# A two-layer DiT trunk on one core: attention by pairs of key tiles, modulation by quads

## The chip, the cores and the metric

The kernel runs on one core of a Trainium2 chip. A core has five engines with queues of their own, each of which works its instructions off in order: TensorE (PE in the profile, with the loads of its stationary operand as PEld), VectorE (DVE), ScalarE (ACT), GpSimd (POOL) and SyncE (SP, which here only issues transfers). The metric is the device time of one execution in microseconds (us); less is better.

## What is computed

The reference is a trunk of two layers over 1024 latent and 256 context tokens of width 1024. In each layer the input is normalised and modulated, projected, and sent through four mixers of 256 columns each (mLSTM, attention with low-rank keys and values, a state-space mixer, an S5 scan); their outputs are concatenated, projected and added, and a convolutional FFN follows. Two parts matter here, cut to their lines:

```python
ml = jnp.split(s_lat @ w_mod[l] + b_mod[l], 6, axis=-1)   # modulation, latent
mc = jnp.split(s_ctx @ w_mod[l] + b_mod[l], 6, axis=-1)   # modulation, context
...
def attend(q, k, v):                                       # 4 heads, q and k of 96, v of 64
    s = jnp.einsum('bqhd,bkhd->bhqk', q, k).astype(jnp.float32) * scale
    p = jax.nn.softmax(s, axis=-1).astype(v.dtype)
    return jnp.einsum('bhqk,bkhd->bqhd', p, v)

yc = attend(qc, kc, vc)            # context queries over 256 context keys
yl = attend(ql, k_all, v_all)      # latent queries over all 1280 keys
```

Layer 1 needs no context output, so its attention has latent queries only.

## The kernel before

Activations lie with features on partitions and tokens along the free axis. All is kept in float32; most products are made of three fp32r matmuls on split operands (a high part and a low part, lines 288 to 290), which pass the array once, while a plain float32 product passes it twice.

**Attention.** `attend` (from line 957) goes over two pairs of heads, the two heads `ho` of a pair, and groups of queries `(t0, w)`: in layer 0 256 context queries, then 512 and 512 latent ones; in layer 1 the latter two. A context group meets two tiles of 128 keys, a latent group ten. Ahead of the groups of head h stands `scores(h + 1)`: the key projection of the next head (`a_pkn`, lines 288 to 290) and the maxima of its scores (`a_pm` on PE, line 949, then a reduction on DVE, `a_mx`, line 950); the negated maximum becomes row 96 of the query operand, so that the exponential needs no further subtraction. For each key tile three matmuls (lines 980 to 982) put the scores of 128 keys and w queries into one PSUM bank `a_pst`, ACT takes the exponential into `a_E` (line 984), and one float32 product (line 985) accumulates `a_po`. Its stationary operand is 128 columns of `a_vt`: 64 of values and 64 of ones, so that one half of the rows of `a_po` is the weighted sum and the other the sum of the weights. At the end of a group ACT copies the two halves out (lines 987 and 988); after the second head of a pair DVE takes the reciprocal (line 990), POOL multiplies (line 991), and the result goes to DRAM.

PSUM's eight banks are three pools: `pd` with two banks (`acc`: projections, maxima), `pa` with three (`a_po` and the scores, which so have two banks in turn) and `pb` with three (mLSTM and modulation).

**Modulation.** `mod` (line 140) takes four tiles of 128 output features. The stationary operand is the 32-column `sc`; four of them stand side by side on the array's columns, and a tile of weights `wm` (512 KB, loaded at line 137) is the moving operand: eight matmuls of 128 columns (line 154) for each tile. ACT copies the four column groups out (line 157, `wms`), and a small product with `msel` adds them up (line 159). Layer 0 makes its first 16 tiles ahead of everything; 48 tiles are made within layer 0's attention and 32 within layer 1's. At each group's start and end `extra()` takes the next word of a list PLAN, whose letters stand for one chunk of mLSTM or four tiles of modulation.

**What sets the order.** The kernel is written for a framework that plans the order of each engine's queue at build time: an instruction that is ready by the planner's costs goes first by its place in the program, or by a priority that the code raises. So mLSTM (`m_...`), modulation and the next head's maxima fall between the score and value matmuls on PE. Both layers have a stretch of some 20 us at the end of attention where nothing of these is left.

## Time and profile before

| | us |
|---|---|
| median of 3 runs | 3469.59 (3468.87 to 3469.73) |
| the profiled execution | 3470.5 |
| its span on the core | 3468.7 |
| PE busy in the span | 3246.6 (94%) |
| DVE, ACT, POOL busy | 2047.4, 1244.0, 1081.7 |
| attention of layer 0, by its place in the span | 541 to 870 |
| attention of layer 1 | 2365 to 2650 |

The profile is of one execution. Its rows give, for groups of instructions, the line of the kernel, the engine, the output and inputs by their names in the program, shapes, busy time and mean time; in the timeline each row is a run of like instructions with its start, and records of PE overlap, since matmuls are pipelined: what one costs is read from the starts of its neighbours, not from its own length. A float32 matmul leaves two records, one for each pass. The granted clock (PEclk) is 1.00 at 2.4 GHz.

### The profile page before, as it was taken

How to read it: one execution, taken by the hardware profiler on the slowest of the kernel's cores; microseconds unless marked ns; L12 is line 12 of the kernel's file. 1: busy time of each engine (PE TensorE's matmuls, PEld its weight loads, DVE VectorE, ACT ScalarE, POOL GpSimd, SP SyncE). 2: the span in 40 equal slices, each digit the busy share in tenths (PEclk: the TensorE clock that was granted, in tenths of full speed). 3: DMA queues.
4: the chain of work that ended last, by engine and by line, in shares of the span. 5: the costliest groups of instructions: out<-in, count | busy, mean ns of one | idle time of the engine just before them, and what ended most of it. 6: DMA issues, size and time to landing. Idle time of an engine off the chain costs nothing.

```text
span 3468.7 us, 49086 instructions
## 1 busy us (share of the span) xinstructions
PE 3246.6 (94%) x18567; PEld 2715.2 (78%) x18598; DVE 2047.4 (59%) x3967; ACT 1244.0 (36%) x2149; POOL 1081.7 (31%) x1043
## 2 busy tenths in 40 slices
PE   7899998999989999998999799998999899999996
PEld 6798896666878888886888789996656788887785
DVE  7858647554485333339778583536544855555655
ACT  4223544334344333333111424534334444444211
POOL 1922324011045444442111020223101375554220
PEclk9899999999999999998999899998999999999998
DMA  5566634236412111225332465544153322223421
GB/s 203 159 200 207 178 104 140 91 115 234 156 62 87 66 68 66 73 79 193 112 104 90 128 203 163 154 120 124 60 196 110 106 89 81 84 84 127 147 73 49
DMA packets 287165, 423.63 MB, mean 122 GB/s; under 512 B 91016, under 2 KB 197200, under 8 KB 286928
## 3 DMA queue, kind: packets, MB, share of 16 engines
q1 hardware_dynamic: 176788, 301.29, 28.2%
q10 hardware_dynamic: 110140, 119.20, 10.3%
q8 instruction: 146, 2.39, 0.3%
q14 instruction: 91, 0.75, 0.1%
HBM read 301.48 MB, written 118.91 MB: 121 GB/s over the span
## 4 chain that ended last, share of the span: by engine, by line
PE 39%; DVE 6%; DMA 2%; issue 2%; ACT 1%; SPq 0%; POOL 0%; ACTq 0%; POOLq 0%; DVEq 0%
PE pd L289 4%; PE pd L290 4%; PE pd L288 4%; PE px L288 2%; PE px L290 2%; PE px L289 2%; PE a_po L985 2%; PE ps_in L289 1%; PE ps_in L288 1%; PE ps_in L290 1%; PE pz L288 1%; PE pz L289 1%; PE pz L290 1%; PE ps_out L289 1%; PE ps_out L288 1%
## 5 line engine op out<-in xcount | busy, mean ns | idle before, releaser
L289 PE MATMUL pd<-fl,wh_d 128*128 128x512 f32 (+1 forms) x896 | 333.5, 374 | 15.2 <-DVE fl L206 15.2
L288 PE MATMUL pd<-fh,wh_d 128*128 128x512 f32 (+1 forms) x896 | 326.9, 374 | 20.0 <-ACT fh L205 12.5
L290 PE MATMUL pd<-fh,wl_d 128*128 128x512 f32 (+1 forms) x896 | 328.4, 371 | 0.0
L206 POOL TENSOR_TENSOR wl_d<-wr_d,wh_d 128x1024 fp32r<-128x1024 f32 x44 | 112.3, 2570 | 461.5 <-ACT wh_d L205 366.7
L1647 DVE SCALAR_TENSOR_TENSOR xx<-pd,modv,xx 128x512 f32<-128x512 f32 (+1 forms) x248 | 165.0, 677 | 121.7 <-PE pd L290 121.0
L288 PE MATMUL ps_in<-ha,wh_in 128*128 128x384 f32 (+3 forms) x688 | 217.7, 326 | 17.0 <-ACT st L1473 16.7
L290 PE MATMUL ps_in<-ha,wl_in 128*128 128x384 f32 (+3 forms) x688 | 223.3, 325 | 0.0
L289 PE MATMUL ps_in<-ha,wh_in 128*128 128x384 f32 (+3 forms) x688 | 223.2, 324 | 0.0
L288 PE MATMUL ps_in<-hc,wh_in 128*128 128x256 f32 (+1 forms) x704 | 215.1, 308 | 6.7 <-ACT hc L220 4.5
L289 PE MATMUL ps_in<-hc,wh_in 128*128 128x256 f32 (+1 forms) x704 | 214.7, 305 | 0.7 <-DVE hc L221 0.7
L290 PE MATMUL ps_in<-hc,wl_in 128*128 128x256 f32 (+1 forms) x704 | 214.0, 304 | 0.0
L288 PEld LDWEIGHTS pd<-fh,wh_d 128*128 128x128 f32 x896 | 171.1, 192 | 53.6 <-ACT fh L205 15.2
L289 PEld LDWEIGHTS pd<-fl,wh_d 128*128 128x128 f32 x896 | 172.3, 193 | 47.1 <-DVE fl L206 19.6
L290 PEld LDWEIGHTS pd<-fh,wl_d 128*128 128x128 f32 x896 | 171.8, 192 | 28.1
L950 DVE TENSOR_REDUCE a_mx<-a_pm 128x1 f32<-128x512 f32 (+1 forms) x200 | 114.6, 591 | 116.7 <-PE a_pm L949 115.1
L985 PE MATMUL a_po<-a_E,a_vt 128*128 128x512 f32 (+1 forms) x336 | 171.1, 595 | 2.9 <-ACT a_E L984 2.5
L206 POOL TENSOR_TENSOR wlo_u<-wr_u,whi_u 128x1024 fp32r<-128x1024 f32 x44 | 106.2, 2415 | 216.2 <-ACT whi_u L205 177.0
L984 ACT ACTIVATE a_E<-a_pst 128x512 f32<-128x512 f32 (+1 forms) x168 | 98.3, 587 | 202.7 <-PE a_pst L982 199.7
L205 ACT CAST wh_d<-wr_d 128x1024 fp32r<-128x1024 f32 x44 | 45.2, 1047 | 299.6 <-PE pd L289 193.9
L288 PEld LDWEIGHTS ps_in<-ha,wh_in 128*128 128x128 f32 x688 | 133.0, 194 | 19.7 <-ACT st L1473 17.1
L288 PEld LDWEIGHTS ps_in<-hc,wh_in 128*128 128x128 f32 x704 | 135.7, 194 | 8.8 <-ACT hc L220 5.6
L206 DVE TENSOR_TENSOR wlo_s<-wr_s,whi_s 128x1024 fp32r<-128x1024 f32 x42 | 71.3, 1697 | 118.2 <-ACT whi_s L205 118.2
(637 smaller groups left out, 9425.1 us busy)
## 6 DMA issues: line engine op xcount, KB each, us to landing
...
```

The costliest lines, as they stand in the source:

```text
L205: nc.scalar.copy(hi, src)
L206: (eng or nc.gpsimd).tensor_tensor(lo, src, hi.bitcast(F32), OP.subtract)
L288: mm(ps, whi(k), ahi(k), start=start and i == 0, stop=False)
L289: mm(ps, whi(k), alo(k), start=False, stop=False)
L290: mm(ps, wlo(k), ahi(k), start=False, stop=stop and i == len(ks) - 1)
L950: nc.vector.tensor_reduce(mx[:, c, j:j + 1], ps[:, :kw], mybir.AxisListType.X, OP.max)
L984: nc.scalar.activation(E[:, :w], ps[:, :w], AF.Exp, scale=scale)
L985: nc.tensor.matmul(po[:, :w], vt[:, kt, hp, 64 * ho:64 * ho + P], E[:, :w], start=kt == 0, stop=kt == kts[-1])
L1647: nc.vector.scalar_tensor_tensor(v, ps, K.modv[l][:, 8 * part + m, c:c + 1], v, OP.mult, OP.add)
```

## The change

In attention two key tiles form a pair. Six score matmuls fill a tile of two PSUM banks, one exponential of 128 x 1024 follows, and the value product becomes two float32 matmuls with 64 stationary columns each, tile i of the pair on columns 64 i to 64 i + 63 and so on rows 64 i of `a_po`. The ones in `a_vt` are gone (64 columns for each head, one copy for a chunk of keys where there were two). The sums of the weights are now added up elementwise: POOL adds the first tile of each pair to `S`, DVE the second; after the second head of a pair of heads `finish` adds the two on DVE, two matmuls with 64 columns of ones sum over the partitions (`a_pr`), DVE takes the reciprocal from PSUM, POOL multiplies. The halves of `a_po` are joined by one ACT copy and one DVE addition. PSUM's pool `pa` is closed and opened anew around attention: one bank for `a_po` and one tile of two banks for the scores, so the scores have no second buffer. In `mod_load4` and `mod` four tiles of modulation are loaded into one tile of 2 MB (two of them instead of four of 512 KB) and multiplied by eight matmuls of 512 columns, issued together; the 16 tiles ahead of layer 0 stay as they were. The value products, `a_pr` and these matmuls have a raised priority.

The core of the diff:

```diff
-        self.pd, self.pa, self.pb = (ctx.enter_context(pool_(tc, name=f"p{i}", bufs=b, space=PSUM)) for i, b in (("d", 2), ("a", 3), ("b", 3)))
+        self.pd, self.pb = (ctx.enter_context(pool_(tc, name=f"p{i}", bufs=b, space=PSUM)) for i, b in (("d", 2), ("b", 3)))
+        self.cpa = None
+        ctx.callback(lambda: self.cpa.close())
+        self.open_pa()
...
+        self.cpa = ExitStack()
+        self.pa = self.cpa.enter_context(pool_(self.tc, name=f"p{name}", bufs=3 if name[0] == "a" else 1, space=PSUM))
...
+    def mod_load4(self, l, js, pool, bufs):
+
+        w = pool.tile([P, 4, KT, P], F32, tag="wm", name=f"wm{l}_{js[0]}", bufs=bufs)
+        for i, j in enumerate(js):
+            self.nc.sync.dma_start(w[:, i], self.A["w_mod"][l, j])
+        return w
...
+            if hasattr(ws, "name"):
+                with self.tc.high_priority(TOGETHER):
+                  for r in range(2):
+                    for g in range(4):
+                        nc.tensor.matmul(ps[32 * g:32 * g + 32, :], self.sc[:, 2 * g + r], ws[:, :, 2 * g + r], start=r == 0, stop=r == 1, skip_group_check=True)
+            for i, j in enumerate(() if hasattr(ws, "name") else js):
...
-        vt = self.vt = late.tile([P, NCH, 2, 192], F32, name=n("vt"))
+        vt = self.vt = late.tile([P, NCH, 4, 64], F32, name=n("vt"))
...
-        nc.gpsimd.memset(vt[:, :, :, 64:128], 1.0)
...
-            for o in range(2):
-                nc.scalar.copy(vt[:, c, :, 128 * o:128 * o + 64], psv[:, :, o])
+            nc.scalar.copy(vt[:, c], ps[:, :256].rearrange("p (h e) -> p h e", h=4))
...
-                    po = K.psm.tile([P, 512], F32, tag="m", name=n(f"po{h}{t0}"))
-                    kts = range(2) if t0 < TC else range(NCH)
-                    for kt in kts:
-                        ks = slice(kt * P, kt * P + P)
-                        ps = K.psm.tile([P, 512], F32, tag="m", name=n(f"pst{h}{t0}{kt}"))
-                        nc.tensor.matmul(ps[:, :w], kh[:97, ks], qh[:97, t0:t0 + w], start=True, stop=False)
-                        nc.tensor.matmul(ps[:, :w], kh[:96, ks], ql[:96, t0:t0 + w], start=False, stop=False)
-                        nc.tensor.matmul(ps[:, :w], kl[:96, ks], qh[:96, t0:t0 + w], start=False, stop=True)
-                        E = epool.tile([P, 512], F32, tag="E", name=n(f"E{h}{t0}{kt}"), bufs=3)
-                        nc.scalar.activation(E[:, :w], ps[:, :w], AF.Exp, scale=scale)
-                        nc.tensor.matmul(po[:, :w], vt[:, kt, hp, 64 * ho:64 * ho + P], E[:, :w], start=kt == 0, stop=kt == kts[-1])
-                    me, ot = slice(64 * ho, 64 * ho + 64), slice(64 - 64 * ho, 128 - 64 * ho)
-                    nc.scalar.copy(y[me, :w], po[me, :w])
-                        nc.vector.reciprocal(r[:, :w], r[:, :w])
-                        nc.gpsimd.tensor_tensor(y[:, :w], y[:, :w], r[:, :w], OP.mult)
-                        y_put(2 + hp, 1, y[:, None, :w], t0, w)
...
+                        ys[t0].append(epool.tile([P, 2, 2, w], F32, tag=f"S{t0}", name=n(f"S{hp}{t0}"), bufs=1))
+                    y, r, S = ys[t0]
+                    po = K.pa.tile([P, 512], F32, tag="m", name=n(f"po{h}{t0}"))
+                    nk = 2 if t0 < TC else NCH
+                    old = None
+
+                    def values(k0, E):
+                        with K.tc.high_priority(TOGETHER):
+                          for i in range(2):
+                            nc.tensor.matmul(po[64 * i:64 * i + 64, :w], vt[:, k0 + i, h], E[:, i, :w], start=k0 == 0, stop=k0 + 2 == nk)
+
+                    for k0 in range(0, nk, 2):
+                        ps = K.pa.tile([P, 2, 512], F32, tag="s", name=n(f"pst{h}{t0}{k0}"))
+                        for i in range(2):
+                            ks = slice((k0 + i) * P, (k0 + i) * P + P)
+                            nc.tensor.matmul(ps[:, i, :w], kh[:97, ks], qh[:97, t0:t0 + w], start=True, stop=False)
+                            nc.tensor.matmul(ps[:, i, :w], kh[:96, ks], ql[:96, t0:t0 + w], start=False, stop=False)
+                            nc.tensor.matmul(ps[:, i, :w], kl[:96, ks], qh[:96, t0:t0 + w], start=False, stop=True)
+                        E = epool.tile([P, 2, 512], F32, tag="E", name=n(f"E{h}{t0}{k0}"), bufs=3)
+                        nc.scalar.activation(E[:, :, :w], ps[:, :, :w], AF.Exp, scale=scale)
+                        if old:
+                            values(*old)
+                        if k0 == 2:
+                            settle()
+                        for i in range(2):
+                            if nk == 2:
+                                eng[i].tensor_copy(S[:, i, ho], E[:, i, :w])
+                            elif k0:
+                                eng[i].tensor_tensor(S[:, i, ho], old[1][:, i, :w] if k0 == 2 else S[:, i, ho], E[:, i, :w], OP.add)
+                        old = k0, E
+                    values(*old)
                     nc.scalar.copy(r[me, :w], po[ot, :w])
-                    nc.scalar.copy(y[me, :w], po[me, :w])
+                    nc.vector.tensor_tensor(y[me, :w], po[me, :w], r[me, :w], OP.add)
+
+                    def finish(h=h, t0=t0, w=w, y=y, r=r, S=S, hp=hp):
+                        ps = K.acc(n(f"pr{h}{t0}"))
+                        nc.vector.tensor_tensor(S[:, 0], S[:, 0], S[:, 1], OP.add)
+                        with K.tc.high_priority(TOGETHER):
+                          for i in range(2):
+                            nc.tensor.matmul(ps[64 * i:64 * i + 64, :w], K.ones[:, :64], S[:, 0, i], start=True, stop=True)
+                        nc.vector.reciprocal(r, ps[:, :w])
+                        nc.gpsimd.tensor_tensor(y, y, r, OP.mult)
+                        y_put(2 + hp, 1, y[:, None, :w], t0, w)
+
+                    settle()
                     if ho:
+                        later.append(finish)
                     extra()
+        settle()
...
-                    ready.append((*q, iter(list(K.mod_load(*q, mw, 4)))))
+                    ready.append((*q, K.mod_load4(*q, mw, 2)))
...
+            K.open_pa(f"t{l}")
             at.attend(ap, ep, y_put, extra)
+            K.open_pa(f"a{l}")
```

**PE, end of layer 0's attention.** No filler is left here; `a_pst` are scores, `a_po` value products. Before:

```order
L985 MATMUL a_po_9221<-a_E_9268,a_vt 128x512
L980 MATMUL a_pst_9278<-a_qh_6611,a_kh_6517 128x512
L981 MATMUL a_pst_9278<-a_ql_6615,a_kh_6517 128x512
L982 MATMUL a_pst_9278<-a_qh_6611,a_kl_6519 128x512
L985 MATMUL a_po_9221<-a_E_9275,a_vt 128x512
L980 MATMUL a_pst_9285<-a_qh_6611,a_kh_6517 128x512
L981 MATMUL a_pst_9285<-a_ql_6615,a_kh_6517 128x512
L982 MATMUL a_pst_9285<-a_qh_6611,a_kl_6519 128x512
L985 MATMUL a_po_9221<-a_E_9282,a_vt 128x512
```

Now (lines 1020 to 1022 are the scores, 1014 the values):

```order
L1014 MATMUL a_po_8783<-a_E_8791,a_vt 64x512 x2
L1020 MATMUL a_pst_8793<-a_qh_6600,a_kh_6517 128x512
L1021 MATMUL a_pst_8793<-a_ql_6604,a_kh_6517 128x512
L1022 MATMUL a_pst_8793<-a_qh_6600,a_kl_6519 128x512
L1020 MATMUL a_pst_8793<-a_qh_6600,a_kh_6517 128x512
L1021 MATMUL a_pst_8793<-a_ql_6604,a_kh_6517 128x512
L1022 MATMUL a_pst_8793<-a_qh_6600,a_kl_6519 128x512
L1014 MATMUL a_po_8783<-a_E_8800,a_vt 64x512 x2
L1020 MATMUL a_pst_8813<-a_qh_6600,a_kh_6517 128x512
```

What one key tile did, six scores and a pair of half-width products do; the values of a pair come right ahead of the next pair's scores.

**PE, modulation in layer 1.** `pm` on line 154 is modulation; the names `wm_34` to `wm_36` are its tiles. Before:

```order
L982 MATMUL a_pst_24943<-a_qh_23134,a_kl_23042 128x512
L154 MATMUL pm_32_24959<-wm_34_24880,sc 32x128 x6
L154 MATMUL pm_32_24959<-wm_35_24882,sc 32x128 x2
L949 MATMUL a_pm_24645<-a_kh_23041,a_qh_23135 128x512
L154 MATMUL pm_32_24959<-wm_35_24882,sc 32x128 x2
L954 MATMUL a_pmr_24639<-cst,a_mx_24598 1x128
L985 MATMUL a_po_24886<-a_E_24940,a_vt 128x512
L980 MATMUL a_pst_24950<-a_qh_23134,a_kh_23040 128x512
L981 MATMUL a_pst_24950<-a_ql_23138,a_kh_23040 128x512
L982 MATMUL a_pst_24950<-a_qh_23134,a_kl_23042 128x512
L154 MATMUL pm_32_24959<-wm_35_24882,sc 32x128 x4
L154 MATMUL pm_36_25008<-wm_36_25000,sc 32x128 x4
```

Now, the same tiles (line 172 is modulation, 183 the product with `msel`, 975 the maxima's transposition, 312 to 314 the key projection):

```order
L172 MATMUL pm_32_24454<-wm_32_24380,sc 32x512 x8
L975 MATMUL a_pmr_23828<-cst,a_mx_23741 1x128
L312 MATMUL a_pkn_24134<-a_kvh,a_wkh 64x432
L313 MATMUL a_pkn_24134<-a_kvl,a_wkh 64x432
L314 MATMUL a_pkn_24134<-a_kvh,a_wkl 64x432
L183 MATMUL pm_32_24454<-msel,wms_32_24463 128x2 x4
L172 MATMUL pm_36_24476<-wm_36_24471,sc 32x512 x8
```

Before, each tile's matmuls stand apart between scores and values; now four tiles go as one block, and several such blocks stand close together.

**PE, the last maxima of layer 0** (line 949 before, 970 now). Before:

```order
L949 MATMUL a_pm_8684<-a_kh_6517,a_qh_6611 128x512
L980 MATMUL a_pst_9174<-a_qh_6611,a_kh_6517 128x512
L981 MATMUL a_pst_9174<-a_ql_6615,a_kh_6517 128x512
L982 MATMUL a_pst_9174<-a_qh_6611,a_kl_6519 128x512
L949 MATMUL a_pm_8687<-a_kh_6517,a_qh_6611 128x512
L159 MATMUL pm_4_8912<-msel,wms_4_8945 128x2 x4
L985 MATMUL a_po_9145<-a_E_9171,a_vt 128x512
L980 MATMUL a_pst_9181<-a_qh_6611,a_kh_6517 128x512
L981 MATMUL a_pst_9181<-a_ql_6615,a_kh_6517 128x512
L982 MATMUL a_pst_9181<-a_qh_6611,a_kl_6519 128x512
L949 MATMUL a_pm_8690<-a_kh_6517,a_qh_6611 128x256
L985 MATMUL a_po_9145<-a_E_9178,a_vt 128x512
```

Now:

```order
L970 MATMUL a_pm_8443<-a_kh_6517,a_qh_6600 128x512
L970 MATMUL a_pm_8446<-a_kh_6517,a_qh_6600 128x512
L970 MATMUL a_pm_8449<-a_kh_6517,a_qh_6600 128x256
L970 MATMUL a_pm_8453<-a_kh_6517,a_qh_6600 128x512
L970 MATMUL a_pm_8456<-a_kh_6517,a_qh_6600 128x512
L970 MATMUL a_pm_8459<-a_kh_6517,a_qh_6600 128x256
L970 MATMUL a_pm_8463<-a_kh_6517,a_qh_6600 128x512
L970 MATMUL a_pm_8466<-a_kh_6517,a_qh_6600 128x512
L970 MATMUL a_pm_8469<-a_kh_6517,a_qh_6600 128x256
L975 MATMUL a_pmr_8473<-cst,a_mx_8374 1x128 x3
L1044 MATMUL a_pr_8498<-a_S_7638,ones 64x512 x2
L975 MATMUL a_pmr_8473<-cst,a_mx_8374 1x128
```

The maxima stood one by one between scores and values, and now stand in one run that ends with the sums `a_pr` (line 1044) and a block of modulation.

## Rows read from the trace of the kernel before

**Rows 1.** windows: start:end, length, busy us (instructions) by engine, granted clock, DMA share, rate.

```profile
541.00:870.00 329.00, 313.23 (x2076) 212.80 (x2084) 189.68 (x405) 133.21 (x272) 57.82 (x62) 0.96 0.43 139
2365.00:2650.00 285.00, 271.36 (x1552) 175.00 (x1561) 155.62 (x326) 113.00 (x214) 43.15 (x44) 0.96 0.37 120
```

**Rows 2.** page, section 5: group | busy us, mean ns | idle before, releaser.

```profile
L950 DVE TENSOR_REDUCE a_mx<-a_pm 128x1 f32<-128x512 f32 (+1 forms) x200 | 114.6, 591 | 116.7 <-PE a_pm L949 115.1
L985 PE MATMUL a_po<-a_E,a_vt 128*128 128x512 f32 (+1 forms) x336 | 171.1, 595 | 2.9 <-ACT a_E L984 2.5
...
L984 ACT ACTIVATE a_E<-a_pst 128x512 f32<-128x512 f32 (+1 forms) x168 | 98.3, 587 | 202.7 <-PE a_pst L982 199.7
```

**Rows 3.** the waits in layer 0: us in total, times, longest.

```profile
PEld a_po L985 <- ACT a_E L984: 3.1, 3, 1.4
```

**Rows 4.** timeline in the end of layer 1: start, length, engine, line, operation.

```profile
2631.74 0.40 PE L982 MATMUL a_pst<-a_qh,a_kl 96*128 96x512 f32 x1
...
2631.97 1.02 PE L985 MATMUL a_po<-a_E,a_vt 128*128 128x512 f32 x2
2632.17 0.60 ACT L984 ACTIVATE a_E<-a_pst 128x512 f32<-128x512 f32 x1 [1.21 <-PE a_pst L982]
...
2632.43 0.80 PE L980 MATMUL a_pst<-a_qh,a_kh 97*128 97x512 f32 x1
...
2633.07 0.39 PE L981 MATMUL a_pst<-a_ql,a_kh 96*128 96x512 f32 x1
```

**Rows 5.** timeline of PE in layer 1, modulation between maxima.

```profile
2532.72 0.43 PE L154 MATMUL pm<-wm,sc 128*32 128x128 f32 x8
2533.07 0.50 PE L949 MATMUL a_pm<-a_kh,a_qh 96*128 96x512 f32 x1
2533.50 0.85 PE L154 MATMUL pm<-wm,sc 128*32 128x128 f32 x20
...
2534.60 0.63 PE L154 MATMUL pm<-wm,sc 128*32 128x128 f32 x12
2535.16 0.33 PE L824 MATMUL m_pf<-cst,m_h 128*128 128x128 f32 x1
2535.41 0.64 PE L154 MATMUL pm<-wm,sc 128*32 128x128 f32 x14
```

**Rows 6.** windows, modulation alone (operands named wm): PE busy (matmul records).

```profile
541.00:870.00 329.00, 34.28 (x768) 22.97 (x768) 0.96 0.43 139
2365.00:2650.00 285.00, 25.71 (x512) 15.09 (x512) 0.96 0.37 120
```

**Rows 7.** timeline of PE, mLSTM products of 64 stationary columns, then the next product.

```profile
526.29 0.66 PE L748 MATMUL m_pu<-m_vw,m_kt 128*64 128x130 f32 x8
526.89 0.44 PE L737 MATMUL m_pt<-cst,m_lk 128*128 128x128 f32 x2
```

**Rows 8.** lines by form: count, ns least/median/most, first and last start.

```profile
L205 ACT CAST wh_d<-wr_d x44: 1031/1047/1056, 1530.2 to 3411.1; 128x1024 fp32r<-128x1024 f32 x44
...
L1760 DVE TENSOR_TENSOR xx<-xx,xr x40: 409/685/2875, 1588.0 to 3233.2; 128x512 f32<-128x512 f32 x32, 128x256 f32<-128x256 f32 x8
...
L1830 POOL TENSOR_TENSOR wr_s<-wr_s,wr_u x42: 1287/2156/2551, 1033.3 to 3135.3; 128x512 f32<-128x512 f32 x42
```

**Rows 9.** timeline, layer 0: last exponential, load for its product, next stage.

```profile
861.50 0.60 ACT L984 ACTIVATE a_E<-a_pst 128x512 f32<-128x512 f32 x1 [0.97 <-PE a_pst L982]
...
862.15 0.30 PEld L985 LDWEIGHTS a_po<-a_E,a_vt 128*128 128x128 f32 x2 [0.72 <-ACT a_E L984]
...
864.98 1.75 PE L288 MATMUL ps_out<-hb,wh_out 128*128 128x256 f32 x4 [1.70 <-ACT hb L205]
```

**Rows 10.** windows after layer 0, and within layer 1; columns as in rows 1.

```profile
865.00:870.00 5.00, 4.98 (x20) 4.19 (x20) 5.00 (x3) 3.90 (x6) 4.64 (x4) 0.66 0.85 304
875.00:880.00 5.00, 2.77 (x13) 1.97 (x14) 2.63 (x2) 3.75 (x6) 3.31 (x3) 1.00 1.04 397
...
2563.00:2573.00 10.00, 9.96 (x49) 6.07 (x48) 5.23 (x12) 4.52 (x7) 0.00 (x0) 1.00 0.90 346
```

14 lines of the change are left out of this document (11 added, 3 removed).

## The prediction

> **What bounds the kernel now.** I read the windows of the two attention stages first: PE is busy 313.2 of 329 us in layer 0 and 271.4 of 285 in layer 1, the next engine, DVE, 189.7 and 155.6 [rows 1]. Then the page's groups and the waits, which say from which side an operation is late: the exponential idles 199.7 us for the scores on PE, the value product idles 2.9 us in all, 3.1 us of waits in layer 0 [rows 2, 3]. So PE sets the time of both stages, ACT is ahead of it, and the change is worth what it takes off PE less the waits it puts there. Outside the stages the instructions are the same. The sum is made against the profiled 3470.5 us; the median lies 0.9 lower.
>
> **Prices on PE.** They are read from starts [rows 4]: the last score matmul and the first value pass are 0.23 apart; from the value product's start to the start of the next second score matmul it is 1.10, so the product's two passes cost 1.10 - 0.23 = 0.87. A key tile costs 3 x 0.23 + 0.87 = 1.56, a pair 3.12. From the last score matmul's start the exponential begins after 0.43 [rows 4], and the load for its product 0.05 after the exponential's end [rows 9]. An exponential of 512 columns takes 0.60 [rows 4]; one of 1024 is not in the trace. It lies between ACT's 1024-column cast, 1.05 [rows 8], and two exponentials, 1.20; I take 1.05, as it is one instruction over the same length.
>
> **Value products.** Do two products on halves of the columns run side by side? Eight passes of mLSTM products with 64 columns and 130 moving elements are followed by the next product after 0.60 us [rows 7]. One pass of 130 costs 0.87 / 1024 x 130 = 0.11, so eight in turn need 0.88 and two abreast 0.44; they run abreast, and about 0.16 is an overhead. What entering and leaving such a block costs shows better in modulation [rows 5]: 2532.72 to 2533.50 is 0.78; two rounds of four (8 records) take 2 x 0.109 and the maximum between 0.235, so 0.33 is left. 2534.60 to 2535.41 leaves 0.81 - 0.33 - 0.11 = 0.37. I take 0.33 (0.16 to 0.37).
>
> The trace shows a loss of about a third of a us for each block that splits the columns [rows 5]. The Trainium skill (TensorEngine Tiling (Array Packing), Key Properties) says that changing the tiling mode drains TensorE, which speaks against many small blocks. By its two-times speedup alone (Theoretical Speedup) a pair would save 0.87 and not 0.54, an estimate from that page that would put the kernel some 28 us lower. The trace agrees with the drain, and the sum does without that page.
>
> A pair then costs 0.87 + 0.33 for its values where two products took 1.74: 0.54 saved, **if other work covers the exponential**. Scores have one buffer, and the values stand right ahead of the next scores, so between the last score and the values PE needs filler of 0.43 + 1.05 + 0.05 - 0.23 = 1.30 us. I counted the filler of each pair in the new PE order at the trace's prices. Of 80 pairs of 512 queries, 56 have it, 7 have part (short by 0.35 on average), and 17 have none: the ends of both stages (8 and 9 pairs), as in the first order fence. Covered: 56 x 0.54 = -30.2. Part: 7 x (0.54 - 0.35) = -1.3. Without cover a pair is 5 x 0.23 + 0.43 + 1.05 + 0.05 + 0.87 + 0.33 = 3.88 against 3.12, so 17 x 0.76 = +12.9. The four context pairs: +0.5.
>
> **Sums of the weights.** `finish` adds ten blocks, eight of 0.87 + 0.33 and two of half the length: +11.1.
>
> **Modulation.** The stages hold 768 and 512 records [rows 6]; at four abreast that is 1280 / 4 x 0.109 = 34.9 us of streaming, and the new matmuls of 512 columns stream the same. What goes are blocks: I count some 43 and 45 runs in the timeline (from 647.3 and 2493.2 on), and 12 and 8 in the new order. 68 x 0.33 = -22.4 (with 0.16 to 0.37: -11 to -25).
>
> The parts on PE come to -29.4.
>
> **What comes back.**
> - The end of layer 0. Before, 33 matmuls of the next stage lie in the last value products, and even so PE waits 1.70 us for ACT's `hb` afterwards [rows 9]. In the new order all of them follow the last values. They are some 6 us at 0.12 to 0.23 each, part of which fills waits for transfers there: +4 (0 to 8). The same in layer 1 stood behind before, too.
> - The runs of maxima (third fence). DVE takes 0.59 for a maximum [rows 2], PE 0.12 to 0.23, and two banks are between them; a run of 14 holds PE some 14 x (0.59 - 0.19) = 5.6 us, less the other work in it. Transfers: in layer 1 the last four quads of modulation are 8.4 MB close together (second fence); the best rate in that stage is 346 GB/s [rows 10], so 24 us against some 22 of PE work between them. Both together +8 (2 to 14): these are the only rows that touch it, so the middle.
> - The additions to `S`: 64 on DVE at 0.69 and 64 on POOL at 1.29 at the least [rows 8], stand in DVE's queue ahead of maxima. 64 x 0.69 = 44 us fit into DVE's 269 idle us of the two stages [rows 1], as do the 8 additions of 1024 columns. POOL is idle most of the time. The exponentials lose their double buffer on PSUM, so an ACT instruction ahead of them now costs PE where it cost nothing. +3 for both (0 to 14; the upper end is the second rival).
> - At no cost: the copies of `a_vt` (ten ACT instructions fewer), the addition of the halves on DVE (some 20 of 0.6), three buffers for `a_E` of twice the size. DVE's idle covers these; if it were the bound they would cost some 10 us.
>
> -29.4 + 15 = -14.4: 3456.1 in a profile, 3455.2 in the median.
>
> **Rivals.**
> - *All covered.* The returns do not arise, since runs of maxima and exponentials' waits hide each other: -29 to -25, so 3440 to 3445. For it: PE waited only 3 us for exponentials though ACT was not idle [rows 3]. Against it: that was with two score buffers.
> - *DVE and POOL block each other.* POOL's addition of 128 x 512 with two SBUF inputs takes 1.29 at its best and 2.16 in the median, DVE's 0.69 in the median and 2.88 at the worst [rows 8], so each has a partner that stretches it. In the change both start right after the same exponential. If DVE's waits for POOL's, 64 x 1.29 = 83 us come on DVE: its share in the stages rises from 56% to (345 + 44 + 83 + 10) / 600 = 80%, and maxima behind an addition are late by up to 2 us. With 40 pairs that have maxima as filler and a quarter of that reaching PE, 40 x 0.5 = 20, of which 3 is in the sum: 3472, no change. The Trainium skill (SBUF — State Buffer, Who interferes with whom) states that a DVE instruction with two SBUF inputs and a GpSimd instruction that reads SBUF hold a shared port pair in turn, each for its whole length; the rows' stretched times agree, and no row shows it for these operations.
> - *PE's clock falls in the ends.* PE then waits about 1.5 us in each of 17 to 24 pairs that are not covered. After 2.5 us of idleness at the end of layer 0 the granted clock was 0.66 over 865 to 870, a mix of 1.2 and 2.4 GHz [rows 10]. At the lower level a pair's 1.15 + 1.20 us of PE work double: +2.35, and 17 to 24 pairs give +40 to +56 us: **slower**, 3495 to 3511, from the point at which more than six of them run so. Against it: over 875 to 880, with PE busy 2.77 of 5 us, the clock stayed 1.00 [rows 10], and in the ends it would be busy about 2.4 of 3.9.
> - *The halves do not run abreast* for 512 moving elements: 84 x 0.87 + 10 x 0.87, +80, 3535. The rows of 130 elements speak against it [rows 7].
>
> **How the numbers follow.** My forecast, 3446 to 3462, has 0.42; all covered (3425 to 3446) 0.17; DVE and POOL (3462 to 3480) 0.24, of which 0.19 lies within 0.2% and 0.05 above it; the clock 0.12; halves in turn 0.02; some other loss 0.03. A measurement of this kernel tells 0.2%, 6.9 us, from no change: faster is below 3462.7, slower above 3476.5. Faster 0.59, same 0.19, slower 0.22. For 8 in 10 the range takes the forecast, DVE and POOL, and most of all covered, 3430 to 3480; it leaves out the clock's case, the halves', the other loss and a little at the lower end.
>
> **What would show it.** In the new profile: value records in pairs a few ns apart, and 0.54 less for a covered pair; an exponential of about 1.05; pairs of 3.9 us in the ends, at a clock of 1.00; 20 blocks of modulation of 1.7 us of streaming each; attention of layer 0 some 6 to 9 us shorter, of layer 1 some 7 to 10. The forecast is wrong if PE waits for `a_E` or for DVE's maxima by more than 15 us outside the ends (DVE and POOL), if the clock in the ends is below 1.00, if an exponential of 1024 takes 1.2 (then +0.15 for each uncovered pair, 3 to 4 us), or if the block's overhead is not 0.33: at 0.16 the values gain 84 x 0.17 = 14 us and modulation loses 12, so this price nearly cancels.

## The result: slower by half a per cent

The changed kernel takes 3486.70 us in the median of 4 runs (3483.78 to 3488.96), the kernel before 3469.23 beside it: a ratio of 1.0055 (1.0037 to 1.0072). It is slower, by more than the 0.2% that a measurement of this kernel can tell, and the prediction, 3455.2 with a range of 3430 to 3480, was wrong. The profiled execution took 3488.96 (span 3487.1), 18.5 more than the one before.

**The profile after.** Windows of the changed kernel, cut where PE goes from one stage to the next, in layer 0 and then in layer 1: the entry (queries, keys, values) from the last matmul of the input projection to the first scores, attention to the last value product, and the output projection to its last matmul. Columns as in [rows 1].

```profile
523.10:588.20 65.10, 44.81 (x222) 30.96 (x221) 53.92 (x84) 28.29 (x78) 33.14 (x35) 0.76 0.53 170
588.20:858.60 270.40, 251.11 (x1291) 146.01 (x1290) 175.67 (x373) 87.33 (x123) 71.56 (x61) 0.93 0.38 133
858.60:988.20 129.60, 122.74 (x697) 104.97 (x694) 74.37 (x101) 47.62 (x80) 26.05 (x21) 0.96 0.41 135
2365.10:2429.90 64.80, 45.55 (x199) 30.42 (x198) 48.64 (x87) 27.07 (x59) 26.09 (x27) 0.79 0.43 135
2429.90:2654.40 224.50, 204.60 (x997) 115.30 (x996) 146.32 (x283) 73.42 (x100) 70.07 (x54) 0.94 0.34 117
2654.40:2748.40 94.00, 92.68 (x492) 78.31 (x489) 61.52 (x77) 36.56 (x57) 16.77 (x13) 0.96 0.42 138
```

The same windows of the kernel before are 51.2, 283.9, 116.0, 57.2, 230.2 and 90.2 us long, with granted clocks of 0.90, 0.98, 0.99, 0.79, 1.00 and 0.98. Its two attention stages:

```profile
578.80:862.70 283.90, 277.23 (x1894) 189.61 (x1902) 146.96 (x343) 105.79 (x194) 29.57 (x35) 0.98 0.43 139
2412.60:2642.80 230.20, 227.87 (x1384) 147.18 (x1390) 110.32 (x247) 85.79 (x150) 22.29 (x23) 1.00 0.35 113
```

So both attention stages did become shorter, by 13.5 and 5.7. But both entries grew by 13.9 and 7.6, and the output projection of layer 0 by 13.6; and the clock, which stood at 0.98 and 1.00 in attention, is 0.93 and 0.94.

Lengths alone hide the reason, since a slow PE counts as a busy one. Each stage is therefore split in three: the time in which PE has no matmul (idle); half of its busy time in the stretches where the granted clock is at 1.2 GHz, which is what these would have saved at 2.4 (lower clock); and the rest, its work at the full clock. The split tells where the time went. It is not the price of the clock alone: where PE waits for DVE, a faster PE would in part have been idle instead.

| us, before -> after | length | idle | lower clock | work |
|---|---|---|---|---|
| entry 0 | 51.2 -> 65.1 | 9.6 -> 20.3 | 4.8 -> 9.1 | 36.8 -> 35.7 |
| attention 0 | 283.9 -> 270.4 | 6.7 -> 19.3 | 6.6 -> 17.5 | 270.6 -> 233.6 |
| output 0 | 116.0 -> 129.6 | 6.3 -> 6.9 | 1.7 -> 4.8 | 107.9 -> 118.0 |
| entry 1 | 57.2 -> 64.8 | 13.3 -> 19.3 | 9.3 -> 9.2 | 34.6 -> 36.3 |
| attention 1 | 230.2 -> 224.5 | 2.3 -> 19.9 | 0.0 -> 11.4 | 227.9 -> 193.2 |
| output 1 | 90.2 -> 94.0 | 2.5 -> 1.3 | 1.7 -> 3.2 | 86.0 -> 89.5 |
| the six | 828.6 -> 848.4 | 40.8 -> 86.9 | 24.1 -> 55.2 | 763.7 -> 706.2 |

The rest of the kernel is 1.3 us shorter, which is no difference between two executions. So **PE's work fell by 57.5 us, and 46.1 of idleness and 31.1 of lower clock took its place.** What follows looks for these two.

**Place one: maxima in a run, then everything late.** Windows of 5 us of the changed kernel, columns as above.

```profile
2585.00:2590.00 5.00, 3.83 (x19) 2.08 (x17) 2.84 (x6) 0.59 (x1) 0.00 (x0) 1.00 0.43 156
2590.00:2595.00 5.00, 4.00 (x8) 1.84 (x8) 4.50 (x10) 1.04 (x1) 0.00 (x0) 0.60 0.27 102
2595.00:2600.00 5.00, 3.93 (x11) 1.61 (x13) 3.12 (x7) 0.00 (x0) 0.00 (x0) 0.50 0.34 105
2600.00:2605.00 5.00, 1.56 (x6) 0.09 (x2) 3.70 (x2) 0.59 (x1) 2.78 (x3) 0.84 0.00 0
```

POOL does nothing for 15 us, DVE is busy 4.50 of 5 in the second row, there the clock falls, and in none of the rows behind is it back at 1.00. The timeline of the same place (idle time before a row, and its releaser, in brackets):

```profile
2590.72 1.13 PE L970 MATMUL a_pm<-a_kh,a_qh 96*128 96x512 f32 x2 [0.44 <-DVE a_mx L971]
...
2599.28 1.98 PE L1044 MATMUL a_pr<-a_S,ones 128*64 128x512 f32 x4
...
2601.30 3.36 DVE L1045 RECIPROCAL a_r<-a_pr 128x512 f32<-128x512 f32 x1 [2.93 <-PE a_pr L1044]
2601.41 1.26 POOL L1033 TENSOR_TENSOR a_S<-a_E,a_E 128x512 f32<-128x512 f32 x1 [31.84 <-PE a_pr L1044]
...
2604.58 0.63 DVE L1033 TENSOR_TENSOR a_S<-a_E,a_E 128x512 f32<-128x512 f32 x1
...
2605.24 3.30 DVE L1033 TENSOR_TENSOR a_S<-a_S,a_E 128x512 f32<-128x512 f32 x2
2605.30 1.02 ACT L1024 ACTIVATE a_E<-a_pst 128x1024 f32<-128x1024 f32 x1 [3.11 <-DVE a_S L1033]
...
2606.38 1.12 PE L1014 MATMUL a_po<-a_E,a_vt 128*64 128x512 f32 x2 [4.81 <-ACT a_E L1024]
```

Read it upwards. PE waits 4.81 us for an exponential; the exponential was not waiting for scores but for DVE's addition to `S`, which still holds its buffer of `a_E`; the addition stood behind a reciprocal of 3.36; that one, and POOL's addition after 31.84 us of nothing, waited for `a_pr`. And `a_pr`, whose inputs had long been there, comes after the whole run of the next head's maxima, in which PE goes at DVE's pace. In layer 0 the same chain ends at 809.61 with a wait of 2.43, after 36.98 us in which POOL waited for `a_pr`.

Why does a product with a raised priority stand behind the maxima (eleven of them in one row on PE, in both layers)? It takes its PSUM tile from `acc`, the pool `pd`, which has two banks, and the maxima take theirs from the same pool. In the planned order `a_pr` gets its bank in its turn in the program's text, behind the maxima of the next head, which were written first. The priority cannot pass that. This is read from the order and the code; an experiment below moves `a_pr` to another pool.

**Place two: the entry.** Timeline of layer 0, DVE, POOL and PE:

```profile
528.79 8.65 DVE L782 SCALAR_TENSOR_TENSOR m_C<-m_C,gm_dp 128x65 f32<-128x65 f32 x4
537.46 0.60 DVE L907 TENSOR_TENSOR a_qt<-a_ps_q,a_tab 96x432 f32<-96x432 f32 x1
```

```profile
530.00 1.05 POOL L768 TENSOR_TENSOR m_vw<-m_vt,gm_ws 128x520 f32<-128x520 f32 x1
531.01 1.10 POOL L230 TENSOR_TENSOR a_ql<-a_qt,a_qh 96x432 fp32r<-96x432 f32 x1
532.07 1.97 POOL L230 TENSOR_TENSOR a_cql<-a_cq,a_cqh 128x848 fp32r<-128x848 f32 x1
534.00 3.16 POOL L230 TENSOR_TENSOR a_kvl<-a_kvf,a_kvh 128x256 fp32r<-128x256 f32 x3
```

```profile
531.11 0.66 PE L772 MATMUL m_pu<-m_vw,m_kt 128*64 128x130 f32 x8
...
538.74 0.72 PE L312 MATMUL a_ps_q<-a_cqh,wh_a_q 128*128 128x424 f32 x1 [6.38 <-DVE a_qr L908]
```

Four updates of mLSTM's state, of 65 columns, take DVE 8.65 us, while POOL works without a pause; PE has nothing to do until DVE has taken the queries out of PSUM, and waits 6.38. In layer 1 there are two such waits, 7.3 and 5.7. By form, the updates are short otherwise (count, ns least/median/most, first and last start; the changed kernel and the one before):

```profile
L782 DVE SCALAR_TENSOR_TENSOR m_C<-m_C,gm_dp x64: 274/284/7028, 528.8 to 2404.4; 128x65 f32<-128x65 f32 x64
```

```profile
L758 DVE SCALAR_TENSOR_TENSOR m_C<-m_C,gm_dp x64: 268/281/3517, 536.5 to 2395.8; 128x65 f32<-128x65 f32 x64
```

Two things of the change lie in the entry: the memset of `a_vt`, 1.17 us on POOL, is gone, and ACT copies the values in ten instructions instead of twenty. The planner's order is another: the next chunk of mLSTM (`m_vw` on POOL, eight `m_pu` on PE) stands before the second half of the queries' inputs. In the kernel before, POOL made `a_cql` first:

```profile
535.12 1.99 POOL L206 TENSOR_TENSOR a_cql<-a_cq,a_cqh 128x848 fp32r<-128x848 f32 x1
...
538.12 1.07 POOL L744 TENSOR_TENSOR m_vw<-m_vt,gm_ws 128x520 f32<-128x520 f32 x1
```

**Place three: the ends.** Timeline of the end of layer 0's attention, and its clock:

```profile
827.38 1.08 PE L1014 MATMUL a_po<-a_E,a_vt 128*64 128x512 f32 x4 [1.17 <-ACT a_E L1024]
...
830.15 1.02 ACT L1024 ACTIVATE a_E<-a_pst 128x1024 f32<-128x1024 f32 x1 [2.83 <-PE a_pst L1022]
...
831.23 1.08 PE L1014 MATMUL a_po<-a_E,a_vt 128*64 128x512 f32 x4 [1.17 <-ACT a_E L1024]
```

```profile
830.00:840.00 10.00, 6.55 (x26) 2.85 (x26) 2.08 (x3) 3.09 (x4) 4.49 (x3) 1.00 0.00 0
```

A pair takes 831.23 - 827.38 = 3.85 us where two tiles took 3.12, at a clock of 1.00. It is what the prediction had said, 3.88. PE's waits for exponentials, where [rows 3] had 3.1 us in layer 0, are now, in attention of layer 0 and of layer 1 (total, times, longest):

```profile
PE a_po L1014 <- ACT a_E L1024: 12.9, 11, 2.4
```

```profile
PE a_po L1014 <- ACT a_E L1024: 14.0, 9, 4.8
```

Less the two long ones of place one these are 19.7 us in 18 waits. Of these 15, 17.2 us, are in the ends (827 to 858 and 2627 to 2654).

### The profile page after: what moved, and what is told of

Read it like the earlier page. It is cut to its first block, busy times and chain, and to the rows that moved or that the text cites. A ratio compares the mean times of both kernels' runs of the same rounds, so it can differ in the third digit from the quotient of the medians.

```text
span 3487.1 us, 47319 instructions
## 1 busy us (share of the span) xinstructions
PE 3223.8 (92%) x17678; PEld 2655.9 (76%) x17678; DVE 2133.4 (61%) x4065; ACT 1217.1 (35%) x2025; POOL 1180.6 (34%) x1109
## 4 chain that ended last, share of the span: by engine, by line
PE 38%; DVE 8%; DMA 3%; ACT 2%; issue 2%; POOL 0%; SPq 0%; ACTq 0%; DVEq 0%; POOLq 0%
PE pd L313 4%; PE pd L314 4%; PE pd L312 4%; PE px L312 2%; PE px L314 2%; PE px L313 2%; PE ps_in L312 1%; PE ps_in L314 1%; PE ps_in L313 1%; PE a_po L1014 1%; PE pz L312 1%; PE pz L313 1%; PE pz L314 1%; PE ps_out L312 1%; PE ps_out L313 1%
## 5 line engine op out<-in xcount | busy, mean ns | idle before, releaser
L312 PE MATMUL pd<-fh,wh_d 128*128 128x512 f32 (+1 forms) x896 | 328.6, 377 | 21.4 <-ACT fh L229 10.1
L312 PE MATMUL ps_in<-ha,wh_in 128*128 128x384 f32 (+3 forms) x688 | 216.7, 325 | 11.8 <-ACT st L1533 11.3
L312 PEld LDWEIGHTS pd<-fh,wh_d 128*128 128x128 f32 x896 | 172.1, 193 | 57.5 <-ACT fh L229 12.8
L1024 ACT ACTIVATE a_E<-a_pst 128x1024 f32<-128x1024 f32 (+1 forms) x84 | 84.3, 1003 | 186.7 <-PE a_pst L1022 165.7
L312 PEld LDWEIGHTS ps_in<-hc,wh_in 128*128 128x128 f32 x704 | 134.9, 192 | 9.7 <-ACT hc L244 5.6
L313 PEld LDWEIGHTS ps_in<-hc,wh_in 128*128 128x128 f32 x704 | 135.3, 192 | 2.6 <-DVE hc L245 1.9
```

Of the source, the lines that this page charges most:

```text
L312: mm(ps, whi(k), ahi(k), start=start and i == 0, stop=False)
L313: mm(ps, whi(k), alo(k), start=False, stop=False)
L1024: nc.scalar.activation(E[:, :, :w], ps[:, :, :w], AF.Exp, scale=scale)
```

## Experiments

All ratios are to the kernel before on the same chip, with a 95% interval. Line numbers of a kernel with an added line are one higher.

**The two halves of the change, each alone.** First attention without the modulation by quads:

```diff
-                    ready.append((*q, K.mod_load4(*q, mw, 2)))
+                    ready.append((*q, iter(list(K.mod_load(*q, mw, 4)))))
```

> The attention part alone: modulation tile by tile as before. Theory 'clock': what the change lost inside attention is not the pairs but the runs of maxima beside the modulation blocks and exponentials held up behind them, with 37 and 27 us at the lower clock; without the blocks the planner's longest run of maxima is 9 and not 14, the time at the lower clock in the two attentions falls below 15 us each, the entries stay slow, and the time is 3470 to 3484. Rival 'structure': the pairs themselves cost more than single key tiles and modulation had paid for part of it; the time is 3492 to 3505.

Measured 3487.72 (3481.57 to 3491.08): 1.0061 (1.0044 to 1.0078). This lies between what the two theories gave. The longest run of maxima is 9, as expected, but attention spends 22.2 and 10.2 us at the lower clock, not less than 15 in each layer. Then the kernel before with nothing but `mod_load4` and the branch in `mod`:

```diff
-                    ready.append((*q, iter(list(K.mod_load(*q, mw, 4)))))
+                    ready.append((*q, K.mod_load4(*q, mw, 2)))
```

> The modulation part alone on the old kernel. Theory 'clock' and the prediction's term agree: some 68 blocks less at 0.33 us, 22 us off PE, less a run of 11 maxima in layer 1 that DVE holds up (5 us, and some 10 us at the lower clock, 5 more): 3452 to 3462, with entries of 51 and 57 us. If the term was mis-sized (a block costs 0.16), 3458 to 3466; if the loads of 2 MB hold PE, above 3469.

Measured 3451.22 (3449.64 to 3455.11): 0.9960 (0.9945 to 0.9975), faster, and a little below the 3452 that was expected at the least. Its attention stages are 279.2 and 225.3 us long.

So attention is the slow half, by some 18 us (21 by its ratio), and modulation is a gain of some 18 (14 by its ratio) that the whole doesn't show. Work on PE in the six stages, by the split above: modulation alone 763.7 -> 741.5, that is -22.2; the predicted term was -22.4. (In the profiled execution some 9 us of the gain are outside the six stages, where nothing changed; the stages became 10.4 shorter, since idleness and clock gave 12 back.) Attention alone, -39.1; the predicted terms were -43.2 + 11.1 = -32.1. Added to attention, modulation takes off another 18.4 of work (724.6 to 706.2), but the loss to the lower clock rises by 20.6 (34.6 to 55.2), and idleness by 3.2. By this split, what modulation takes off PE beside attention comes back as a slower PE.

**Place one: a bank for the sums from another pool.** One line:

```diff
-                        ps = K.acc(n(f"pr{h}{t0}"))
+                        ps = K.pb.tile([P, 512], F32, tag="m", name=n(f"pr{h}{t0}"))
```

> The changed kernel with one line other: the product that sums the weights (a_pr) takes its PSUM bank from the pool of mLSTM and modulation (pb) and not from the one of the maxima (pd). Theory 'bank': banks of a pool are handed out in the program's order, so a_pr must wait until the next head's 14 remaining maxima have been through; the sums S, the buffers a_E and the next exponential wait for it (2.4 and 4.8 us in one place of each layer), PE meanwhile goes at DVE's pace through the maxima and its clock falls for 20 to 24 us. Then the runs of maxima vanish, time at the lower clock in the two attentions falls from 37 and 27 us to below 15 and 8, and the kernel gains 22 to 33 us: 3454 to 3465. Rival: the low clock comes from the uncovered ends or from the long modulation blocks; it stays, the gain is under 12 and the time over 3475.

Measured 3451.55 (3448.66 to 3461.32, 8 runs): 0.9951 (0.9938 to 0.9963). One line takes 35 us off the median of the changed kernel, somewhat more than was expected, and makes it faster than the one before. (Its profiled execution, 3461.3, is the slowest of the eight; its six stages are 26.5 us shorter.) Windows of its attention stages:

```profile
591.20:841.80 250.60, 240.51 (x1290) 141.20 (x1290) 176.76 (x373) 87.01 (x123) 72.33 (x61) 0.97 0.42 144
...
2416.50:2630.90 214.40, 201.00 (x996) 114.47 (x996) 145.31 (x284) 73.69 (x100) 69.10 (x53) 0.97 0.34 120
```

They are 19.8 and 10.1 shorter: idleness falls from 39.2 to 23.5, the loss to the lower clock from 28.9 to 14.6, and work stays (426.8 and 426.9). The time at the lower clock falls from 36.7 and 27.3 us to 16.2 and 13.7, not quite as far as expected. In the timeline `a_pr` now stands among the maxima, and no row of five or more maxima is left on PE:

```profile
2500.75 0.51 PE L970 MATMUL a_pm<-a_kh,a_qh 96*128 96x256 f32 x2
...
2502.14 1.08 PE L1044 MATMUL a_pr<-a_S,ones 128*64 128x512 f32 x4
2503.15 0.50 PE L970 MATMUL a_pm<-a_kh,a_qh 96*128 96x512 f32 x1
```

and POOL's additions (line 1033) sat idle for `a_pr` far less; the changed kernel first, then this one (us, times):

```profile
  PE a_pr L1044: 82.1, 4
```

```profile
  PE a_pr L1044: 15.9, 2
```

The longest wait of PE for an exponential is 1.2 here, not 4.8. That is the chain of place one, cut at its first link. (The line also leaves both banks of `pd` to the maxima; no run tells that apart from the earlier place of `a_pr`.)

**Place three: two banks and two exponentials again.** The scores of each tile in a bank of their own, an exponential of 512 columns for each; the values still as two halves side by side. The second tile's half now goes first, and the first tile's is tied to it; no run has the banks without this.

```diff
-                          for i in range(2):
-                            nc.tensor.matmul(po[64 * i:64 * i + 64, :w], vt[:, k0 + i, h], E[:, i, :w], start=k0 == 0, stop=k0 + 2 == nk)
+                          for i in (1, 0):
+                            m = nc.tensor.matmul(po[64 * i:64 * i + 64, :w], vt[:, k0 + i, h], E[:, i, :w], start=k0 == 0, stop=k0 + 2 == nk)
...
+                                K.tc.add_manual_dep(m.ins, m1.ins.name, NOSYNC, reason="halves together")
...
-                        ps = K.pa.tile([P, 2, 512], F32, tag="s", name=n(f"pst{h}{t0}{k0}"))
+                        E = epool.tile([P, 2, 512], F32, tag="E", name=n(f"E{h}{t0}{k0}"), bufs=3)
                         for i in range(2):
+                            ps = K.pa.tile([P, 512], F32, tag="m", name=n(f"pst{h}{t0}{k0 + i}"))
...
-                        nc.scalar.activation(E[:, :, :w], ps[:, :, :w], AF.Exp, scale=scale)
+                            nc.scalar.activation(E[:, i, :w], ps[:, :w], AF.Exp, scale=scale)
...
-            K.open_pa(f"t{l}")
...
-            K.open_pa(f"a{l}")
```

> The changed kernel, with each key tile's scores in a bank of its own and an exponential of 512 of its own, as before the change; the values still go in halves, two tiles together. The next scores can then start while the second exponential runs. If the single exponential's exposed wait is what the ends lose (1.16 us in each of some 17 pairs), a pair in the ends goes from 3.84 to about 2.7 us and the time falls by 17 to 20 us, to 3465 to 3470. Theory 'clock' adds that the two long waits for exponentials (2.4 and 4.8 us) and the low clock around the runs of maxima stay, since a_E is still held by the sums. Rival: the blocks of halves are dear by themselves, a pair stays above 3.2 us and the time above 3478.

Measured 3467.18 (3460.98 to 3473.89, 10 runs): 0.9995 (0.9984 to 1.0006), 19.5 below the changed kernel and within what was expected. In layer 0's end a pair now takes 2.67 us instead of 3.85:

```profile
827.03 1.08 PE L1014 MATMUL a_po<-a_E,a_vt 128*64 128x512 f32 x4
...
829.70 1.08 PE L1014 MATMUL a_po<-a_E,a_vt 128*64 128x512 f32 x4
```

In the two attention stages PE's idleness falls from 39.2 to 21.6, by as much as the ends' 17.2, while `a_pr` still follows the last maxima, with waits of 2.1 and 4.2 us behind it. So the one exponential for two tiles with its single buffer, which the change is named for, costs 20 us here, and some 13 and 16 in the mended kernels below. ACT was not the bound; the pair of scores takes the bank that was the second buffer, and PE pays for it.

**Place two: three attempts.** The old stream of the entry, with the ones written to a tile that nothing reads, and two copies for a chunk of values:

```diff
+        one = pk.tile([P, NCH, 2, 64], F32, name=n("one"))
+        nc.gpsimd.memset(one, 1.0)
         for c in range(NCH):
...
-            nc.scalar.copy(vt[:, c], ps[:, :256].rearrange("p (h e) -> p h e", h=4))
+            psv = ps[:, :256].rearrange("p (a h e) -> p a h e", a=2, h=2)
+            for o in range(2):
+                nc.scalar.copy(vt[:, c, o::2], psv[:, :, o])
```

> The changed kernel, with the old entry's instructions put back: POOL's memset of 128 x 1280 (into a scratch tile) and two ACT copies per chunk of values where the change has one. Theory 'entry': from the end of the input projection to the first score matmul the changed kernel needs 65.1 and 64.8 us where the old one needed 51.2 and 57.2, because DVE's updates of the mLSTM state (m_C) stand behind POOL's work; if the missing memset and copies brought that about, both entries come back to 51 to 58 us and the time is 3465 to 3473. Rival: the shift has another source (the planner's order), both entries stay at 63 to 66 us and the time at 3484 to 3489.

Measured 3481.93 (3480.61 to 3486.89): 1.0049 (1.0034 to 1.0064), entry 0 59.8 long and entry 1 66.7, so neither of the two expectations fits. The memset of the extra tile stands later in POOL's queue than the old one did, and at the place shown above the old order did not come back: the four updates take 8.65 us again, and PE waits 6.39. Of the 5.3 us by which entry 0 is shorter 4.1 are the loss to the lower clock. This run says nothing for or against the memset. Next, the updates of `m_C` alone: all of them stand behind the queries in the program's text (`chain`), and in layer 0 the first four also wait for the third part of the queries.

```diff
+                    m = nc.vector.scalar_tensor_tensor(C[:, cn, q, d], C[:, c, q, d], g.m_dec[:, d, c, q:q + 1], C[:, cn, q, d], OP.mult, OP.add)
+                    if i == 1 and l in (0,):
+                        K.tc.add_manual_dep(m.ins, K.qr[2].ins.name, NOSYNC, reason="after the queries")
...
                 at.queries(late, mp)
+            K.chain()
```

> The changed kernel with the first four updates of the mLSTM state on DVE (m_C) put behind the third query tile in layer 0, as in the old order; layer 1 is left. Theory 'entry': there an update waits 7.0 us on DVE while POOL reads SBUF, and PE waits 6.4 us behind it for the queries; the entry of layer 0 goes from 65 to 52 to 57 us, the time to 3474 to 3480. Rival: DVE waits as long at another place, the entry stays at 62 to 66 and the time at 3482 to 3489.

Measured 3486.27 (3469.40 to 3488.53, 10 runs): 1.0039 (1.0023 to 1.0054). Entry 0 is 65.0 long, as before the edit: the rival's case. DVE is held in the new place too, 7.34 us for the four; PE's longest wait for the queries falls from 6.4 to 3.4 and the idleness by 2.8, but the loss to the lower clock rises by 2.8. So the place of these updates alone doesn't settle the entry's length. Last, one line that computes nothing that is needed (the copies overwrite all of it): the memset back on the tile and at the place where it had been.

```diff
         nc.sync.dma_start(wv, A["w_uv"][l])
+        nc.gpsimd.memset(vt[:, :, 0:2], 1.0)
         for c in range(NCH):
```

> The changed kernel plus one instruction without use: POOL writes ones over 128 x 1280 of a_vt ahead of the copies that fill it, as POOL wrote the old kernel's ones. In the first try of this the memset went to scratch memory that came free later, so it stood later in POOL's queue; here it stands where the old one stood, and the planned order of the entry of layer 0 is the old one again on PE, DVE and POOL. Theory 'order': without the memset the planner lets mLSTM's next chunk (m_vw on POOL, m_pu on PE) go ahead of the queries' operands, and that is what made the entry slow; the entry of layer 0 goes from 65 to 52 to 56 us; layer 1, whose order is not quite the old one, from 65 to 57 to 65. Time 3466 to 3478. Rival: the entry's length has nothing to do with that order, stays at 60 to 65 in layer 0, and the time is above 3480.

Measured 3465.40 (3463.51 to 3472.10, 10 runs): 0.9996 (0.9985 to 1.0007), 21 us below the changed kernel, and just below the 3466 that was expected at the least. The window of entry 0, and PE and DVE in its timeline:

```profile
525.80:581.90 56.10, 41.47 (x222) 28.24 (x221) 47.65 (x81) 27.71 (x78) 34.91 (x35) 0.89 0.60 191
```

```profile
534.33 0.43 PE L312 MATMUL a_ps_q<-a_cqh,wh_a_q 128*128 128x424 f32 x1 [1.27 <-DVE a_qr L908]
534.92 0.72 PE L313 MATMUL a_ps_q<-a_cql,wh_a_q 128*128 128x424 f32 x1 [0.15 <-POOL a_cql L230]
```

```profile
534.22 5.97 DVE L782 SCALAR_TENSOR_TENSOR m_C<-m_C,gm_dp 128x65 f32<-128x65 f32 x3
```

DVE is held here too, for 5.97 us, as it was in the kernel before. But `a_cql` was made before that, PE has eleven products in hand meanwhile, and its wait is 1.27, not 6.38. Entry 0 is 9.0 shorter, 56.1 where 52 to 56 was expected; entry 1 stays (65.9). Of the 20 us in the six stages another 9.6 lie in attention of layer 1, where the loss to the lower clock falls from 11.4 to 2.8. The planner's order is another there too: 16 more matmul records stand in entry 1, and a block of modulation stands within what was the run of maxima.

```profile
2570.94 0.83 PE L971 MATMUL a_pm<-a_kh,a_qh 96*128 96x512 f32 x2 [0.67 <-DVE a_mx L972]
2571.70 1.92 PE L172 MATMUL pm<-wm,sc 128*32 128x512 f32 x16
```

```profile
2570.00:2575.00 5.00, 4.12 (x28) 1.71 (x26) 4.64 (x10) 1.63 (x2) 0.00 (x0) 1.00 0.12 46
```

PE has 28 matmul records in these 5 us, where it had 8 in the row at 2590 of the changed kernel, and the longest row of maxima is 5, not 11. The clock held there; it is 0.95 over 2575 to 2580 and 0.50 only over 2580 to 2585, behind `a_pr`. So this half of the 20 us came with another order in layer 1, and not by the entry of layer 0; what in that order keeps the clock is not tested.

**Put together.** The bank and the later updates; these and two banks for the scores; the bank and the memset; these and two banks. The edits are those above. In the table the last four columns are of the profiled execution alone.

> Both of the two runs before it at once. If the two losses are separate they add: 3442 to 3455. If one low clock merely takes the place of another, the time stays above 3460.

> As the run before it, and the scores of the two tiles of a pair in banks of their own with two exponentials of 512. The ends' 17 pairs lose their wait of 1.16 us, and the covered pairs their waits behind ACT: 15 to 22 us below the run before it, 3424 to 3438, faster than the old kernel and than modulation alone (3451). Rival: without the long waits the single exponential costs little more than two, and the gain is under 8 us.

> The memset back, and the product of the sums in its own bank as in the run with that line alone (3451.6). If the two are separate the entry's 9 to 14 us come off that: 3436 to 3444. If the low clock only moves on, no more than 4 us come off: above 3447.

> As the run before it with the scores of a pair in two banks and two exponentials of 512. With the bank alone against the bank, the update and two banks the gain of the two banks was some 11 to 13 us; so 3424 to 3434. If the single exponential costs nothing where its wait is not repeated, it equals the run before it within 4 us.

| kernel | us, median (range, runs) | ratio (95%) | six stages | idle | lower clock | work |
|---|---|---|---|---|---|---|
| before | 3469.23 (4) | 1 | 828.6 | 40.8 | 24.1 | 763.7 |
| changed | 3486.70 (3483.78 to 3488.96, 4) | 1.0055 | 848.4 | 86.9 | 55.2 | 706.2 |
| attention alone | 3487.72 | 1.0061 | 842.8 | 83.7 | 34.6 | 724.6 |
| modulation alone | 3451.22 | 0.9960 | 818.2 | 47.9 | 28.9 | 741.5 |
| two banks for the scores | 3467.18 | 0.9995 | 831.7 | 73.8 | 48.5 | 709.6 |
| memset | 3465.40 | 0.9996 | 828.4 | 83.4 | 35.3 | 709.7 |
| bank for the sums | 3451.55 | 0.9951 | 821.9 | 74.0 | 40.7 | 707.2 |
| bank, later updates | 3453.77 (3449.33 to 3457.05, 6) | 0.9957 (0.9942 to 0.9971) | 807.8 | 68.7 | 31.6 | 707.4 |
| these and two banks | 3440.59 (3437.39 to 3448.91, 4) | 0.9925 (0.9901 to 0.9948) | 809.4 | 63.0 | 41.2 | 705.2 |
| bank and memset | 3447.84 (3435.33 to 3454.99, 5) | 0.9945 (0.9920 to 0.9971) | 804.2 | 70.2 | 25.6 | 708.4 |
| bank, memset, two banks | **3431.72** (3428.49 to 3438.36, 4) | **0.9904** (0.9880 to 0.9929) | 787.7 | 60.4 | 18.5 | 708.8 |

The work column is the change's own gain, and no mending touches it: 705 to 710 in every version with both halves. Everything else is idleness and clock. Stages of different kernels compare only roughly, since one execution stands for each: the profiled one is 12.5 us below the median of its kernel for the bank and the memset, 8.3 above it for the kernel with later updates and two banks, and what lies outside the six stages takes 2629 to 2643 us in these executions. The later updates add nothing to the bank, as they added nothing alone: 3453.77 lies in the range that was expected of a sum, but the bank alone gives it. The bank and the memset, 35 and 21 us apart from each other, are 39 together, not 56, and this kernel's runs are spread over 20 us. Separate gains were expected to give 3436 to 3444; 3447.84 is the case in which at most 4 us come off. That the two gains overlap is measured, in which part is not. The two banks are worth 13 (15 to 22 were expected) and 16 on top, though the intervals of each two kernels compared overlap. The last kernel beats both: 1.0% below the one before, 55 us below the changed one, and its attention stages are 242.2 and 203.1 long, where the kernel before has 283.9 and 230.2:

```profile
584.10:826.30 242.20, 234.90 (x1280) 139.28 (x1290) 173.41 (x376) 93.80 (x167) 70.07 (x61) 0.99 0.43 150
...
2394.00:2597.10 203.10, 196.02 (x968) 111.15 (x972) 137.40 (x273) 79.55 (x139) 63.97 (x53) 0.97 0.36 128
```

## Why the prediction was wrong

**The prices on PE were right.** Before the returns the sum had -43.2 for 80 pairs of values, +11.1 for the sums' blocks and -22.4 for modulation: -54.5 of work; the trace has -57.5. Modulation alone is -22.2 against -22.4; attention alone is -39.1 against -32.1, and the two overlap by 3.8, so part of the agreement is luck. The exponential of 1024 columns takes 1.02 (1.05 was taken), and the pair in the ends 3.85 (3.88). The halves run abreast, so that rival falls: the four passes of a pair's values take 1.08 us in the rows of place three, where four passes in turn at the prediction's price would take 1.74. For modulation by form:

```profile
L172 PE MATMUL pm<-wm,sc x320: 592/592/1063, 646.3 to 2578.5; 128*32 128x512 f32 x160
```

Modulation is 320 records, 20 blocks of four abreast, as the prediction wanted to see; this row was 1280 records in [rows 6].

**Step that failed first: the run of maxima was priced by its holding alone, and the clock at nothing outside the ends.** The term was 14 x (0.59 - 0.19) = 5.6 us, in the +8 with the transfers. It had neither the chain behind `a_pr` nor a lower clock. One line that takes `a_pr` out of the maxima's pool makes the kernel 35 us faster; with it 15.7 us of idleness and 14.3 of lower clock go from attention. The rival that had the clock put it into the ends, at 40 to 56 us; there it stayed at 1.00, as the prediction argued from 875 to 880 [rows 10]. (The idleness that it names at the end of layer 0, 2.5 us, is 1.70 before the next product in [rows 9].) By the split the loss to the lower clock rose by 31.1 us, 22.3 of them in attention; the two stretches of the run and what follows it (793 to 822 and 2589 to 2620) hold 19.2, two thirds of that behind the run. Of the 33 us between forecast and profile the 31.1 are nearly all, but how much of them a faster PE would have kept is not known, since it waits for DVE there. The Trainium skill (TensorE: Matmul & The Clock Gate, HAM oscillation) tells of a clock that falls in a gap in which TensorE waits for a transfer. Here the trace differs in kind: the clock fell within 2590 to 2595, in the run of maxima, and in the ten us before that PE was never idle for longer than 0.67 us.

**Step that failed second: "at no cost" for the entry.** The prediction went through `a_vt`'s copies and not through its memset, and it argued from busy time: POOL is idle most of the time. But the memset's 1.17 us had a place in POOL's queue, and the planner filled that place with something that pushed `a_cql` back. "Outside the stages the instructions are the same" left it out as well: the memset began at 527.97, ahead of the window from 541. The entries' idleness rose by 16.7; the sum had 0 there. The memset's return brings entry 0 from 65.1 to 56.1, against 51.2 before; entry 1 stays, and why is not settled.

**Step that was mis-sized: the end of layer 0.** +4 (0 to 8) was the term, for 33 matmuls; output 0 took on 10.1 us of work, namely 48 matmuls that had been in attention's cover before and the last `a_pr`, and 3.1 of clock. The work itself is no loss, it is in the -57.5, but the stage starts with it at the lower clock.

**What was right for another reason: the idleness in attention.** The steps that cost waits there add up to 22.1 for the ends (17 x 1.30), 2.5 for the pairs with part of the cover, 0.5, 8 and 3: 36. The table has +30.2. The ends are 17.2 of it. With `a_pr` in another pool 15.7 go, and with two banks for the scores 17.6; so the rest is in the main the chain behind `a_pr`, and not the transfers. So the attention stages became 13.5 and 5.7 shorter, near the 6 to 9 and 7 to 10 of the prediction, by other items. This chain was in the third fence to be read: `a_pr` behind all the maxima. The prediction saw a run of maxima there, and didn't ask who waits for what ends it.

**DVE and POOL do stretch each other; what that costs is not isolated.** By form (count, ns least/median/most):

```profile
L1033 POOL TENSOR_TENSOR a_S<-a_S,a_E x48: 1259/1626/2065, 617.2 to 2654.0; 128x512 f32<-128x512 f32 x48
L1033 DVE TENSOR_TENSOR a_S<-a_S,a_E x48: 672/693/1794, 617.6 to 2653.9; 128x512 f32<-128x512 f32 x48
```

DVE's 64 additions take 62.6 us, where 64 x 0.69 would be 44: 18 us are above the median, not the 83 of the rival. With the bank moved the durations are alike (66.1 us in all), and the kernel is 35 us faster, so they are not what makes the changed kernel slow. Whether a few us of them reach PE, in the additions of 3.30 at 2605.24 for one, no run shows.
